# A hybrid decoder layer on one core: third buffers for a pair's operands, a later gate for the turned keys, and fewer small steps

## The chip, the cores and the metric

The kernel runs on one core of one Trainium2 chip. A core has TensorE (PE, with weight loads in a row of their own, PEld), VectorE (DVE), ScalarE (ACT), GpSimd (POOL) and SyncE (SP, which here issues nearly all DMAs). The metric is the device time of one execution in microseconds, the median of several runs; less is better. One further execution is profiled, and all rows come from it.

## The reference

One layer on 512 tokens of width 2048, all in f32. The input projection feeds three mixers side by side: differential attention (4 heads), sliding-window attention (8 query heads), and an RWKV-7 mixer (16 heads of 64). An output projection, a SwiGLU network of hidden width 5632 and a last norm follow. What the change touches is the RWKV recurrence:

```python
def step(S, inp):
    r_t, w_t, k_t, v_t, a_t, b_t = inp
    sa = jnp.einsum('bhvk,bhk->bhv', S, a_t)
    S = S * w_t[:, :, None, :] + sa[..., None] * b_t[:, :, None, :] + v_t[..., None] * k_t[:, :, None, :]
    return S, jnp.einsum('bhvk,bhk->bhv', S, r_t)
...
h = rms_norm(x, attn_norm_g[l]); proj = h @ w_in[l]
x = x + jnp.concatenate([ya, yb, yc], axis=-1) @ w_out[l]
gate, up = _split(rms_norm(x, ffn_norm_g[l]) @ w_gate_up[l], [FFN_HIDDEN, FFN_HIDDEN])
x = x + (jax.nn.silu(gate) * up) @ w_down[l]
```

## The kernel before

**Dense work.** Features lie on the partitions, the 512 tokens along the free dimension. A dense item is one output tile of 128 features: 16 k-tiles, each as three matmuls of 128x128 by 128x512 (high and low parts of both operands, type fp32r), 48 in all (`dense`, `dense_k`, L215 to L223). `sequence` (L348) runs the items in a fixed order and requests the weights of the next item before it runs one: two loads of 512 KB on SP, a split into high and low on ACT (L208) and DVE (L209). The order is r-, k- and v-tiles of eight head pairs (k first), the attention tiles, the output projection, the FFN.

**Small work.** The recurrence is done in chunks of 64 tokens, for a pair of heads (128 features) at a time. For pair `hp` these generators do it:

- `rates` (L457): decay and learning-rate tiles, from two small loads (`w2`, `a2`).
- `prep` (L494): norm of the keys (`kn`), the tile `bk` of scaled keys, the turned keys `bkn` (eight transposes, `bt`, L536 to L543), the tile `ar` with the scaled a and r operands (L547), the products `gr` (16 matmuls for each half of the chunks, L562), which DVE masks into `L`, `zl` and `gr` (L577); then four DMAs `li` (L588), the turned values `vt` (L598) and a bonus term `bon` (L609).
- `inverse` (L616): reads 32x32 triangular blocks back from DRAM and inverts them in 31 steps of two DVE operations, then writes them out (`xi`).
- `join` (L647): after a pause reads the inverted blocks into `L` (L653), after a second pause joins them by 32x32 matmuls (`px`, `pt`, `po`).
- `chain` (L688): eight chunks one after the other, each with small matmuls `z`, `u`, `S` (state) and `y`, and copies on ACT and DVE between them.
- `post` (L739): group norm (`var`), gate (`g`) and the store of the pair's output.

**The order.** All is planned when the program is written. Each generator stands in one of eight lanes, and `pump` (L163) is called after every dense matmul: it advances the first generator of each lane whose due time has come. `yield 7` means 7 planned microseconds; a bare `yield` means until the outputs of the step should be done, plus 0.3. `self.now` counts planned PE time. A wait for another generator is a loop that polls with bare yields. PE keeps exactly the order in which its instructions were written (`keep_in_program_order`); the other engines' instructions are ordered by a scheduler that keeps the dependencies. `need` (L181) pumps without dense work until a named generator is done.

**Buffers.** PSUM pool `pm` has two buffers (`kn`, `bt`, `gr`, `vt`, `bon`, scores), `pc` three, `py` one. In SBUF `ar`, `zl`, `gr`, `bkn`, `uv` and the inverse tiles `linv` exist twice. So `prep` of pair `hp` waits at L534 until the chain of pair `hp-2` has ended, before it turns the keys and goes on to `ar` and `gr`:

```python
while hp >= 2 and f"loop{hp - 2}" not in self.done:
    yield
bkn = rp.tile([P, NCH, P], F32, tag="bkn", name=f"bkn{hp}", bufs=2)
```

## Time and profile before

| | |
|---|---|
| runs, us | 2465.7, 2465.69, 2463.95 (median 2465.69) |
| profiled execution, us | 2460.77 |
| its span, us | 2459.0 |
| mean granted PE clock | 0.994 |
| mixers, to the first output projection | 0 to 805 us |
| output projection | 805 to 1000 us |
| FFN and last norm | 1000 to 2459 us |

The profile gives for each engine its busy time, and for each instruction its start, its length and what it waited for. "Waits" lists who waited for whom, with total, number and longest. "Windows" gives the busy time of the engines (and the number of their instructions) in stretches of time, with the granted clock of PE (1.00 is full), the DMA engines' share and GB/s. "Timeline" gives instructions in order of time: start, length, engine, line, operation, tiles, shapes, number; a bracket gives the idle time before and what ended it. In groups of instructions the columns are the number, the busy time, the mean in ns, and the idle time before. Matmuls are pipelined: their lengths overlap, and the distance of two starts is what one costs.

### The profile page before, as it was taken

What the parts mean: (1) busy time and instruction counts of PE and PEld (TensorE: products, weight loads), DVE (VectorE), ACT (ScalarE), POOL (GpSimd) and SP (SyncE); (2) the same over time, 40 slices, a digit from 0 to 9 for tenths busy, and PEclk for the clock granted to TensorE, in tenths of its full rate; (3) what the DMA queues carried; (4) which work ended last, traced back from release to release, by engine and by line L of the source; (5) the groups of instructions that cost most, each with busy time, mean ns of one, the idle gap of its engine ahead of it and who ended that gap; (6) DMA issues with size and microseconds to landing.
All of it is one profiled execution on the core that took longest, in us unless ns stands there. A gap on an engine that the chain in (4) does not pass through costs nothing.

```text
span 2459.0 us, 30832 instructions
## 1 busy us (share of the span) xinstructions
PE 2415.4 (98%) x12328; PEld 1915.2 (78%) x12328; DVE 1181.9 (48%) x2121; ACT 813.8 (33%) x1391; POOL 99.4 (4%) x157
## 2 busy tenths in 40 slices
PE   8999999999999999999999999999999999999997
PEld 6766666676677778888888888888888888888887
DVE  7567776675544544434343434343434333343437
ACT  5445555444434423322222122222222222222224
POOL 3000000000000003100000000000000000000006
PEclk9999999999999999999999999999999999999999
DMA  5222222222223433222322322322232232232224
GB/s 176 91 77 75 84 75 83 66 82 85 90 86 100 146 124 103 95 95 97 101 95 95 101 96 94 99 98 95 96 101 94 95 101 96 94 100 98 94 96 136
DMA packets 103793, 240.04 MB, mean 98 GB/s; under 512 B 34906, under 2 KB 43746, under 8 KB 103650
## 3 DMA queue, kind: packets, MB, share of 16 engines
q1 hardware_dynamic: 98754, 231.39, 29.4%
q10 hardware_dynamic: 4896, 6.69, 0.8%
q8 instruction: 97, 1.59, 0.3%
q14 instruction: 46, 0.38, 0.0%
HBM read 227.55 MB, written 10.49 MB: 97 GB/s over the span
## 4 chain that ended last, share of the span: by engine, by line
PE 87%; DVE 2%; ACT 1%; DMA 1%; issue 1%; SPq 0%; POOL 0%; DVEq 0%; ACTq 0%; POOLq 0%
PE pg L131 19%; PE pu L131 19%; PE pd L131 19%; PE po L131 7%; PE pd_v L131 3%; PE pd_k L131 2%; PE pd_r L131 2%; PE pd_va L131 2%; PE pd_qa L131 2%; PE pd_qb L131 2%; PE pd_ka L131 1%; PE y L131 1%; PE z L131 1%; PE S L131 1%; PE pd_kb L131 1%
## 5 line engine op out<-in xcount | busy, mean ns | idle before, releaser
L131 PE MATMUL pd<-al,wh_wd 128*128 128x512 f32 (+1 forms) x768 | 285.3, 371 | 0.6 <-DVE al L1141 0.6
L131 PE MATMUL pd<-ah,wh_wd 128*128 128x512 f32 (+1 forms) x768 | 285.5, 372 | 0.4 <-DVE y L1160 0.4
L131 PE MATMUL pd<-ah,wl_wd 128*128 128x512 f32 (+1 forms) x768 | 285.2, 371 | 0.0
L131 PE MATMUL pu<-x1h,wh_wu 128*128 128x512 f32 x704 | 274.3, 390 | 0.0
L131 PE MATMUL pu<-x1l,wh_wu 128*128 128x512 f32 x704 | 273.9, 389 | 0.0
L131 PE MATMUL pu<-x1h,wl_wu 128*128 128x512 f32 x704 | 273.9, 389 | 0.0
L131 PE MATMUL pg<-x1h,wl_wg 128*128 128x512 f32 x704 | 273.9, 389 | 0.0
L131 PE MATMUL pg<-x1l,wh_wg 128*128 128x512 f32 x704 | 273.9, 389 | 0.0
L131 PE MATMUL pg<-x1h,wh_wg 128*128 128x512 f32 x704 | 273.9, 389 | 0.0
L1160 DVE TENSOR_TENSOR y<-y,pd 128x512 f32<-128x512 f32 (+1 forms) x192 | 122.5, 641 | 207.8 <-PE pd L131 207.6
L208 ACT CAST wh_wd<-raw_wd 128x1024 fp32r<-128x1024 f32 x96 | 101.0, 1052 | 356.9 <-PE pd L131 177.2
L208 ACT CAST wh_wu<-raw_wu 128x1024 fp32r<-128x1024 f32 x88 | 92.7, 1053 | 366.7 <-PE pu L131 144.8
L208 ACT CAST wh_wg<-raw_wg 128x1024 fp32r<-128x1024 f32 x88 | 92.7, 1054 | 362.8 <-PE pg L131 144.9
L209 DVE TENSOR_TENSOR wl_wg<-raw_wg,wh_wg 128x1024 fp32r<-128x1024 f32 x88 | 107.8, 1225 | 171.4 <-ACT wh_wg L208 171.4
L209 DVE TENSOR_TENSOR wl_wu<-raw_wu,wh_wu 128x1024 fp32r<-128x1024 f32 x88 | 107.8, 1225 | 133.5 <-ACT wh_wu L208 133.5
L131 PEld LDWEIGHTS pd<-al,wh_wd 128*128 128x128 f32 x768 | 144.7, 188 | 25.7 <-DVE al L1141 0.8
L131 PEld LDWEIGHTS pd<-ah,wh_wd 128*128 128x128 f32 x768 | 144.7, 188 | 25.6 <-issue 0.5
L131 PEld LDWEIGHTS pd<-ah,wl_wd 128*128 128x128 f32 x768 | 144.7, 188 | 24.9
L131 PEld LDWEIGHTS pu<-x1h,wh_wu 128*128 128x128 f32 x704 | 132.1, 188 | 27.6 <-issue 0.2
L131 PEld LDWEIGHTS pu<-x1l,wh_wu 128*128 128x128 f32 x704 | 132.1, 188 | 27.6 <-issue 0.2
L131 PEld LDWEIGHTS pu<-x1h,wl_wu 128*128 128x128 f32 x704 | 132.1, 188 | 27.5
L131 PEld LDWEIGHTS pg<-x1h,wl_wg 128*128 128x128 f32 x704 | 132.1, 188 | 27.4
(357 smaller groups left out, 4100.4 us busy)
## 6 DMA issues: line engine op xcount, KB each, us to landing
raw_wd<-in_w_down SPq DMA_DIRECT2D x96, 512.0 KB, 3.2
raw_wg<-in_w_gate SPq DMA_DIRECT2D x88, 512.0 KB, 3.7
raw_wu<-in_w_up SPq DMA_DIRECT2D x88, 512.0 KB
raw_wo<-in_w_out SPq DMA_DIRECT2D x32, 512.0 KB, 3.5
raw_k<-in_w_in SPq DMA_DIRECT2D x16, 512.0 KB, 3.8
raw_r<-in_w_in SPq DMA_DIRECT2D x16, 512.0 KB, 4.3
raw_v<-in_w_in SPq DMA_DIRECT2D x16, 512.0 KB, 3.7
x<-in_xT SPq DMA_DIRECT2D x16, 256.0 KB, 4.9
```

The lines of the kernel that those rows point to most:

```text
L131: self.tc.keep_in_program_order(self.nc.tensor.matmul(out, lhsT, rhs, start=start, stop=stop))
L208: nc.scalar.copy(out=hi[:, :kn * m], in_=s)
L209: nc.vector.tensor_tensor(out=lo[:, :kn * m], in0=s, in1=hi[:, :kn * m].bitcast(F32), op=ALU.subtract)
L1160: nc.vector.tensor_tensor(out=o, in0=o, in1=ps, op=ALU.add)
```

## The change

- `ar` (a- and r-operands) and `zl` (the small chain's operand) become one tile `Z` with three planes, held three times; `gr` and `linv` are held three times too. The two ACT copies into `zl` go; DVE writes the a-operand in two halves.
- `prep` now forms `Z` and `gr` first. The keys are turned behind it, and wait only until the chain of `hp-2` has issued its last state matmul (`keys`, chunk 6); the values wait for that chain's end. With two keys blocks in one step, the gr half in one step without a pause in its middle, `bon` in the step of `vt`, and `g` in the step of `var`.
- `join` pauses 8 and 10 in place of 7 and 6.
- Waits are conditions that `pump` tests at its start, in place of polling. A chain starts only when its pair's `prep` has ended.
- Buffers: `w2`/`a2`/`rkm` three in place of four, `g2` one in place of two; `pts` shares a buffer with `xnn`; `keep` has its own; the attention's score tiles, its turned weights and the reloaded mixer outputs lie in `i2`, in a `gr` buffer and in `linv`.

```diff
+        for lane in self.order:
+            if lane:
+                name = lane[0][0]
+                if name in self.until and self.until[name]():
+                    del self.until[name]
+                    self.due[name] = self.now
+                self.due.setdefault(name, self.now)
...
-        self.linv = [lp.tile([P, NCH, P], F32, name=f"linv{j}") for j in range(2)]
+        self.linv = [lp.tile([P, NCH, P], F32, name=f"linv{j}") for j in range(3)]
...
-        while hp >= 2 and f"loop{hp - 2}" not in self.done:
-            yield
-        bkn = rp.tile([P, NCH, P], F32, tag="bkn", name=f"bkn{hp}", bufs=2)
-        for u in range(2):
-            ps = self.pm.tile([P, 4, P], F32, tag="m", name=f"bt{hp}_{u}")
-            for n in range(4):
-                self.tr(ps[:, n, :], bk[:, u * 4 + n].rearrange("p a c -> p (a c)"))
-            nc.scalar.copy(out=bkn[:, u * 4:u * 4 + 4, :], in_=ps)
-            yield
...
+        Z = rp.tile([P, NCH, 3, C], F32, tag="Z", name=f"Z{hp}", bufs=3)
+        for h in range(2):
+            s = HALF[h]
+            nc.vector.scalar_tensor_tensor(out=Z[s, :, h, :], in0=c3(kk)[s], scalar=-1.0, in1=W[s, :, 0:64],
+                                           op0=ALU.mult, op1=ALU.mult)
+        nc.vector.tensor_tensor(out=Z[:, :, 2, :], in0=c3(r), in1=W[:, :, 1:65], op=ALU.mult)
...
-                    self.mm(ps[h][:, j, :], bk[HALF[h], n], ar[HALF[h], n], start=True, stop=True)
-                if j == 1:
-                    yield 0.4
+                    self.mm(ps[h][:, j, :], bk[HALF[h], n], Z[HALF[h], n, h::2 - h], start=True, stop=True)
...
         self.lanes[1].append((f"sub{hp}", self.inverse(q)))
-        while "v" not in q:
-            yield
+
+        if hp >= 2 and f"keys{hp - 2}" not in self.done:
+            yield lambda: f"keys{hp - 2}" in self.done
+        bkn = rp.tile([P, NCH, P], F32, tag="bkn", name=f"bkn{hp}", bufs=2)
+        for u in range(2):
+            ps = self.pm.tile([P, 4, P], F32, tag="m", name=f"bt{hp}_{u}")
+            for n in range(4):
+                self.tr(ps[:, n, :], bk[:, u * 4 + n].rearrange("p a c -> p (a c)"))
+            nc.scalar.copy(out=bkn[:, u * 4:u * 4 + 4, :], in_=ps)
+        yield
+        q["bkn"] = bkn
+        if hp >= 2 and f"loop{hp - 2}" not in self.done:
+            yield lambda: f"loop{hp - 2}" in self.done
+        if "v" not in q:
+            yield lambda: not ("v" not in q)
...
-        yield 7
+        yield 8.0
         for h, b, bl in blocks:
             nc.sync.dma_start(out=L[bl, :, bl], in_=d[h, b].rearrange("n i g t -> (i g) n t"))
-        yield 6
+        yield 10.0
...
+                if n == NCH - 2:
+                    self.done.add(f"keys{hp}")
...
         nc.scalar.activation(sq, sq, AF.Exp, scale=-0.5)
-        yield
+        ps = self.pc.tile([P, T], F32, tag="c", name=f"g{hp}")
+        for j in range(2):
+            self.mm(ps, q["g2"][:, j, :], self.gl[j], start=(j == 0), stop=(j == 1))
         nc.vector.tensor_tensor(out=sq, in0=py, in1=sq, op=ALU.mult)
         self.done.add(f"y{hp}")
```

## The prediction

> **What bounds the kernel now.** I read the head of the page first. Its columns are busy time, share of the span, number of instructions.

> ```profile
> span 2459.0 us, 30832 instructions
> PE 2415.4 (98%) x12328; PEld 1915.2 (78%) x12328; DVE 1181.9 (48%) x2121; ACT 813.8 (33%) x1391; POOL 99.4 (4%) x157
> ```

> PE is the bound. PE runs in the order in which the program wrote its instructions, and the change leaves the number and shapes of the matmuls as they are. So the time can change in three ways only: PE's idle time, the clock at which PE runs, and the cost of switching between the long projection and the small steps. The chain that ended last gives the pace of undisturbed dense work, and where the untouched part begins:

> ```profile
> 1000.14 10.89 PE pg L131 x48
> ```

> 48 matmuls in 10.89 us are 0.227 us each. From 1000 us on the program is the same before and after; everything below lies in the first 1000 us. PE's waits (total, times, longest) are the second view:

> ```profile
> PE px L131 <- DMA linv<-xi: 9.7, 7, 2.9
> PE pd_l L131 <- ACT hl L311: 7.9, 3, 5.5
> ...
> PE bt L135 <- DVE bk L531: 2.3, 1, 2.3
> PE pd_k L131 <- DVE wl_k L209: 2.2, 1, 2.2
> ```

> pd_l is the loading at the start, which stays. The largest wait that the change can reach is px: the join of a pair waits for the inverted blocks to come back through DRAM. The third view, 50-us windows, ends each row with PEclk, the DMA share and GB/s:

> ```profile
> 50.00:100.00 50.00, 47.71 (x209) 38.19 (x208) 30.27 (x41) 29.88 (x43) 4.46 (x21) 1.00 0.26 83
> 100.00:150.00 50.00, 47.79 (x233) 36.60 (x231) 37.16 (x98) 21.17 (x32) 0.41 (x4) 1.00 0.30 91
> 150.00:200.00 50.00, 46.31 (x356) 32.00 (x355) 31.08 (x84) 25.37 (x63) 1.05 (x8) 0.93 0.26 73
> ...
> 450.00:500.00 50.00, 46.68 (x335) 32.80 (x333) 27.86 (x78) 24.34 (x54) 0.83 (x6) 0.90 0.25 69
> ...
> 550.00:600.00 50.00, 47.52 (x370) 32.39 (x369) 27.72 (x94) 22.51 (x62) 0.00 (x0) 0.97 0.29 89
> ```

> The three windows with a clock below 1.00 are those of the three long px waits. Lost: 50 x (0.07 + 0.10 + 0.03) = 3.5 + 5.0 + 1.5 = 10.0 us. The single waits of 2.3 us (bt) and 2.2 us (pd_k) lie in the first two windows and left the clock at 1.00. So px costs 9.7 + 10.0 us, and an idle stretch a little above 2.3 us is enough to lower the clock.

> **The change, part by part.**

> *The join's pauses, 7 and 6 to 8 and 10.* They are planned microseconds. On the first pair SP and PE show what they must cover (the last row is pair 7's):

> ```profile
> 150.73 2.64 SPq L642 DMA_DIRECT2D xi<-xy  x4
> 154.83 1.82 SPq L653 DMA_DIRECT2D linv<-xi  x4
> ```

> ```profile
> 156.67 0.28 PE L131 MATMUL px<-cc,linv 32*32 32x32 f32 x2 [2.95 <-DMA linv<-xi]
> 157.52 1.06 PE L131 MATMUL px<-cc,linv 32*32 32x32 f32 x30 [0.57 <-DMA linv<-xi]
> ...
> 582.27 1.04 PE L131 MATMUL px<-cc,linv 32*32 32x32 f32 x32 [2.37 <-DMA linv<-xi]
> ```

> The wait is 3.5 us at its worst and the plan gets 5 us more. I take all of px out, -9.7, and its clock, -10.0. Bounds: nothing of it, if the inverse ends later against the plan than now, to all of it. The join's four DMAs and its small matmuls come 5 us later; nothing but the pair's own chain waits for them, which today sits idle between pairs.

> *Merged steps.* A step between dense matmuls has an entry and an exit:

> ```profile
> 215.33 0.39 PE L131 MATMUL pd_k<-xl,wh_k 128*128 128x512 f32 x1
> 215.65 0.71 PE L131 MATMUL gr<-ar,bk 64*128 64x128 f32 x8
> 216.30 0.50 PE L131 MATMUL pd_k<-xh,wl_k 128*128 128x512 f32 x1
> 216.63 0.40 PE L131 MATMUL pd_k<-xh,wh_k 128*128 128x512 f32 x1
> ```

> Entry 0.32 - 0.227 = 0.09, exit 0.33 - 0.227 = 0.10: 0.2 us a switch. The gr steps lose 16 of them (3.2 us); the two bt steps and vt with bon lose one each per pair, at about 0.1 (a step of 128 rows enters without a pause): 1.6 us. Together -4.8 (rows of such a step at 328.95 to 329.53 below). Joining g to var I cost at nothing: four 512-column matmuls hide their switch.

> *The gate.* Now prep turns the keys (bt) before it forms gr, and bt waits until the chain of two pairs before has ended:

> ```profile
> 260.38 0.40 PE L131 MATMUL pd_k<-xh,wh_k 128*128 128x512 f32 x1
> ...
> 299.67 0.40 PE L131 MATMUL pd_r<-xh,wl_r 128*128 128x512 f32 x1
> ...
> 318.01 0.39 PE L131 MATMUL pd_k<-xh,wh_k 128*128 128x512 f32 x1
> ...
> 328.34 0.34 PE L131 MATMUL y<-gr,uv 128*64 128x64 f32 x4
> ...
> 328.95 0.39 PE L131 MATMUL pd_k<-xl,wh_k 128*128 128x512 f32 x1
> 329.18 0.60 PE L135 MATMUL bt<-cc,bk 128*128 128x128 f32 x4
> 329.53 0.48 PE L131 MATMUL pd_k<-xh,wl_k 128*128 128x512 f32 x1
> ...
> 406.72 0.69 PE L131 MATMUL px<-cc,linv 32*32 32x32 f32 x32
> ...
> 447.49 0.34 PE L131 MATMUL S<-uv,bkn 128*64 128x64 f32 x4
> ```

> These are pair 4 (k, its last r, its bt, its px, its seventh S), the next pair's k, and the last y of pair 2 that lets bt go. r was ready at 300, gr ended only at 346 (below). Behind the new gate gr would end some 12 us after r, near 312: some 30 us earlier, with four li DMAs on SP, the inverse and the chain behind it. That by itself buys nothing: PE has dense work meanwhile, and does the same work earlier.

> But it decides where bt stands. In the new order bt follows the last gr block, with a pause between only if the seventh S of the chain two pairs before isn't written yet. From gr's end to that S pass 447.49 - 346.14 = 101 us, with the join's pauses 106. Two pairs take 2 x (318.01 - 260.38) = 115 us. So the S is 9 us ahead, no pause is made, and bt stands on PE directly behind gr. Both use the two buffers of the PSUM pool pm. What bt then waits for:

> ```profile
> 345.49 0.72 PE L131 MATMUL gr<-ar,bk 64*128 64x128 f32 x8
> 346.14 0.50 PE L131 MATMUL pd_r<-xh,wl_r 128*128 128x512 f32 x1
> ```

> ```profile
> 346.24 0.42 DVE L577 TENSOR_TENSOR linv<-gr,cc 64x256 f32<-64x256 f32 x1 [0.49 <-PE gr L131]
> ...
> 347.13 0.42 DVE L577 TENSOR_TENSOR gr<-gr,cc 128x256 f32<-128x256 f32 x1
> ...
> 348.38 0.41 DVE L577 TENSOR_TENSOR gr<-gr,cc 128x256 f32<-128x256 f32 x1
> ```

> gr leaves PE free at 346.14. The first buffer is free after DVE's third operation, 347.55; four transposes take 0.35 (329.18 to 329.53); the second buffer is free at 348.79. So bt ends at 349.2, where it would have ended at 346.85 without the wait: **2.35 us** a pair, as two gaps of 1.4 and 0.9 us. Behind bt on PE is the dense stream. Pairs 0 and 1 have no gate and pay for sure; pairs 3 to 7 by the 9 us. Pair 2 I take to have its pause: chain 0 starts behind its px, at 157 now, and from px to the seventh S pass 41 us (406.72 to 447.49), while pair 2's gr no longer waits for that chain. 7 x 2.35 = +16.5. Bounds: two pairs, +4.7, up to seven with one weight split (1.22 us, next fence) ahead of them on DVE, +25.

> *The clock behind it.* The two gaps hold 2.3 us idle within 2.7, just where single waits of 2.2 and 2.3 us did nothing and 2.4 (the px of 582 us, whose clock fell least) did. I take a fall in four pairs at the smallest of the three, 1.5: +6.0. Bounds 0 and 7 x 5.0. [...]

> *vt waits for v.* vt now comes as soon as v's last operation is written down, by the plan some 0.45 us later (a pause of 0.3 and the next dense step), and that operation takes 0.75:

> ```profile
> L209 DVE TENSOR_TENSOR wl_r<-raw_r,wh_r 128x1024 fp32r<-128x1024 f32 x16 | 19.5, 1222 | 6.0 <-ACT wh_r L208 6.0
> ...
> L365 DVE SCALAR_TENSOR_TENSOR v<-h_v,cols,v 128x512 f32<-128x512 f32 x8 | 6.0, 746 | 0.0
> ```

> 0.3 x 6 pairs = +1.8; bounds 0 and 6 x 0.75 = 4.5.

> *At nothing:* the zl copies leave ACT, and one DVE operation of half height comes per pair; the page has both engines under half busy. Waits by condition in place of polling shift steps by at most 0.3 us. One g2 buffer makes its load wait for the g matmuls of the pair before, and the weight loads behind it on SP with it: they are issued a whole item of 10.9 us ahead, else each would cost PE that delay. The li DMAs, now earlier, meet other loads on SP; behind them only the inverse waits. The third buffers take away waits that planned pauses already cover, and the other renamed tiles change neighbours that are long done.

> **Sum:** -9.7 - 10.0 - 4.8 + 16.5 + 6.0 + 1.8 = **-0.2 us**. The profiled execution took 2460.8 us (2459.0 its span), 4.9 below the median of the runs, 2465.7; the difference is carried to the median: **2465.5 us**.

> **The rivals.**
> 1. *The clock falls behind every merged stall, at the mean of the three falls now* (3.3 us): 7 x 3.3 = 23.3 in place of 6.0. **Slower**, 2482.8 us. For it: little dense work stands around the gaps (gr, half the rows, before; transposes between). Against: two waits of 2.2 and 2.3 us left the clock alone. It decides from about 11 us of falls in all.
> 2. *The gate holds bt back*: chains run later than the 9 us allow, as DVE and SP serve them late; then pairs 2 to 7 have their pause, two pairs pay 4.7, one fall 1.5: -24.5 + 4.7 + 1.5 + 1.8 = -16.5, **2449.2 us**. For it: the margin is small against 106. Against: DVE is lighter when gr and inverse no longer crowd one another.
> 3. *px still waits*, because the inverse falls further behind the plan: 19.7 stay, **2485 us**. Against: 1.5 us of reserve even on the worst pair.
> 4. *Short gaps leave the clock alone*: the 6.0 go, **2459.5 us**. For it: the waits of 2.2 and 2.3 us. Against: the three falls. [...]
> 5. *The gate brings no earlier start* because r is late as well: then only px and merges count, the place of bt is that of rival 2, and so is the time.

> **Chances.** Forecast 0.40 (own range 2459 to 2472), rival 1 0.16, rivals 2 and 5 0.25, rival 3 0.07, rival 4 0.12. A measurement of this kernel can tell about 0.2%, 4.9 us, from no change. Faster: a quarter of the forecast's 0.40, nearly all of rivals 2 and 5, two thirds of rival 4: 0.10 + 0.24 + 0.08 = 0.42. Slower: 0.10 + 0.15 + 0.07 = 0.32. The rest, 0.26, is the same. The range goes from a little below rival 2 to rival 1: 2446 to 2483; rival 3 and the outer parts of 1 and 2 are left out, under 0.2.

> **What would show it.** px gone from PE's waits, or under 2 us; a new wait of bt on DVE's gr, some 14 to 17 us over seven pairs; PEclk of 1.00 at the joins and short dips behind gr; gr some 12 us behind r from pair 2 on; chain 7 ending before 600 us. If bt shows no such wait, or vt and gr show more than 5 us, the sum is wrong.

## The result and the profile after

| | before | after |
|---|---|---|
| median of the runs, us | 2465.69 (2463.95 to 2466.34) | 2451.97 (2451.28 to 2453.27) |
| profiled execution, us | 2460.77 | 2452.63 |
| its span, us | 2459.0 | 2450.8 |
| mean granted PE clock | 0.994 | 0.996 |

The changed kernel takes 0.9946 of the time before, 95% interval 0.9929 to 0.9963: 13.7 us less between the medians, 8.1 us between the two profiled executions. The forecast was 2465.5.

In the chain of the changed kernel that ended last (start, length, engine, tile) the FFN begins 8.3 us earlier:

```profile
991.84 10.89 PE pg L132 x48
```

From there to the end it is 2450.8 - 991.8 = 1459.0 us against 2459.0 - 1000.1 = 1458.9 before. So everything lies in the first part, as expected. PE's waits of the changed kernel (total, times, longest):

```profile
PE pd_l L132 <- ACT hl L321: 7.2, 2, 5.6
PE bt L136 <- DVE gr L574: 4.8, 3, 1.8
PE wt L136 <- DVE pa L891: 4.1, 5, 1.3
PE pa L132 <- ACT sg L385: 2.7, 4, 0.7
PE z L132 <- ACT uv L612: 2.1, 3, 1.1
PE bt L136 <- ACT bkn L596: 2.0, 3, 0.7
PE gr L132 <- DVE xt L645: 1.5, 2, 0.8
```

px is gone from the list. In its place stands bt behind DVE's gr, but three times and not seven. Below it are waits that weren't foreseen: z and pa of `rates`, which share the two buffers of `pm` with vt and bon (z waits until ACT has copied vt into uv, pa until ACT has read z's tile for sg), and the attention's turned weights wt behind DVE's pa (2.8 before). The windows, in the columns explained above:

```profile
100.00:150.00 50.00, 45.98 (x225) 35.84 (x224) 37.58 (x100) 19.09 (x30) 0.41 (x4) 0.97 0.26 79
150.00:200.00 50.00, 45.92 (x320) 33.98 (x317) 37.10 (x104) 23.50 (x47) 1.05 (x8) 0.93 0.30 85
...
450.00:500.00 50.00, 49.20 (x369) 33.97 (x367) 39.36 (x108) 29.36 (x65) 0.85 (x6) 1.00 0.23 70
...
550.00:600.00 50.00, 50.00 (x407) 34.63 (x407) 18.51 (x48) 24.98 (x73) 0.00 (x0) 1.00 0.24 75
```

The low clock at 450 to 500 and 550 to 600 us is gone with px. The first row is new: it holds pair 0's bt. PE's timeline there:

```profile
100.22 1.16 PE L132 MATMUL gr<-Z,bk 64*128 64x128 f32 x16
102.87 0.63 PE L136 MATMUL bt<-cc,bk 128*128 128x128 f32 x4 [1.49 <-DVE gr L574]
104.17 1.04 PE L136 MATMUL bt<-cc,bk 128*128 128x128 f32 x4 [0.68 <-ACT bkn L596]
104.86 0.78 PE L132 MATMUL pd_k<-xh,wl_k 128*128 128x512 f32 x1
```

bt stands directly behind gr and waits in two gaps, 1.49 + 0.68 = 2.17 us. The second is put down to ACT's copy of the first block, not to DVE. From 104.3 us on PE runs at half clock, as narrower windows show:

```profile
100.90:104.30 3.40, 1.24 (x15) 0.83 (x12) 2.87 (x7) 0.59 (x1) 0.00 (x0) 1.00 0.51 153
104.31:107.72 3.41, 3.41 (x11) 2.83 (x11) 0.00 (x0) 0.59 (x1) 0.00 (x0) 0.50 0.50 99
107.73:111.00 3.27, 3.27 (x18) 2.71 (x17) 0.16 (x1) 0.39 (x1) 0.00 (x0) 1.00 0.35 100
```

The fall lasts 3.41 us; in it the dense matmuls start 0.43 us apart, behind it 0.23, so about half of it is lost. Behind pair 1's bt it lasts twice as long, 6.83 us (152.09 to 158.91); behind pair 4's there is none (1.00 from 300 to 350 us).

**Where the time went.** I summed PE's gaps of over 0.06 us up to the FFN (those of pd_l at the start apart), half of the time at half clock, and took the remainder as work with its switches. Before: gaps 21.2, clock 10.2, work 960.3 us; after: 22.9, 5.1, 956.3. So gaps +1.7, clock -5.1, work -4.0, and 0.7 less of pd_l's gaps at the start: -8.1. PE hardly waits less than before; it waits in other places, in shorter gaps.

### The profile page after: what moved, and what is told of

It reads as the page before. It is cut to its first block, busy times and chain, and to the rows that moved or that the text cites. A ratio compares the mean times of both kernels' runs of the same rounds, so it can differ in the third digit from the quotient of the medians.

```text
span 2450.8 us, 30872 instructions
## 1 busy us (share of the span) xinstructions
PE 2406.4 (98%) x12328; PEld 1914.4 (78%) x12328; DVE 1184.6 (48%) x2129; ACT 808.1 (33%) x1375; POOL 100.0 (4%) x158
## 4 chain that ended last, share of the span: by engine, by line
PE 79%; DVE 2%; ACT 1%; issue 1%; POOL 0%; DMA 0%; DVEq 0%; ACTq 0%
PE pg L132 20%; PE pu L132 20%; PE pd L132 19%; PE po L132 7%; PE pd_ka L132 2%; PE pd_qa L132 2%; PE pd_va L132 2%; PE pd_qb L132 2%; PE pd_v L132 1%; PE pd_k L132 1%; PE pd_r L132 0%; PE y L132 0%; PE z L132 0%; PE pd_vb L132 0%; PE sb L132 0%
## 5 line engine op out<-in xcount | busy, mean ns | idle before, releaser
L132 PEld LDWEIGHTS pg<-x1h,wh_wg 128*128 128x128 f32 x704 | 132.1, 188 | 27.5
```

The source lines that it names most:

```text
L132: self.tc.keep_in_program_order(self.nc.tensor.matmul(out, lhsT, rhs, start=start, stop=stop))
```

## The experiments

The kernel before, on the same chips, had medians of 2467.0 us (first four runs below), 2467.2 (next four) and 2467.1 (last two). The ratios are to these. The changed kernel wasn't run again beside them; with it, the kernel before had 2465.7, so a difference to the changed kernel is good to some 1.5 us.

**1. The pauses alone.** The kernel before with the new pauses:

```diff
-        yield 7
+        yield 8.0
...
-        yield 6
+        yield 10.0
```

> The kernel before with one edit, the join's pauses 8 and 10. Theory A (the pauses hide the way through DRAM): PE's px waits fall from 9.7 us to under 1 and the clock stays at 1.00 at the joins, 10 to 20 us faster than before (2446 to 2456). Theory B (what ended the px waits in the changed kernel is the new order, which spreads the planned inverse): px still waits 4 us or more here, under 8 us faster.

2465.92 us, ratio 0.9990 (0.9979 to 1.0001): no change. A wait of its profile:

```profile
PE px L131 <- DMA linv<-xi: 6.6, 4, 3.9
```

Fewer px waits than the 9.7 us before, not none, and the granted clock was still 0.70 from 500 to 550 us and 0.98 from 550 to 600. So 5 us more of pause didn't cure px in the old order.

**2. The new order with the old pauses.** The changed kernel with 7 and 6:

```diff
-        yield 8.0
+        yield 7.0
...
-        yield 10.0
+        yield 6.0
```

> The changed kernel with the join's pauses back at 7 and 6. Theory A: px waits 5 us or more again and the clock falls at a join, 2457 us or more. Theory B: no px wait above 0.5 us, since in the changed kernel px stands 13 us or more behind the inverse's last operation and needs 7; the time stays at 2452, plus or minus 3.

2442.26 us, ratio 0.9903 (0.9887 to 0.9918): 9.7 us faster than the changed kernel. px isn't among its waits; bt is, less often:

```profile
PE pa L132 <- ACT sg L385: 3.4, 5, 0.7
PE bt L136 <- DVE gr L574: 3.3, 2, 1.8
...
PE bt L136 <- ACT bkn L596: 1.4, 2, 0.7
```

px is cured here without the pauses: the new order does it (which part of it, the third buffers or the later gate, no run separates). In the changed kernel px comes 13 to 38 us behind the inverse's last DVE operation, here 14 to 45, before 6 to 12; where it waited before, the way through DRAM took 6 to 8. The time was missed, because I expected the pauses to be neutral. They move every later step of a pair against the others: with the old ones pair 4's bt is held back and stalls no more. In the profiles PE's gaps are 6.6 us less, of which bt is 2.2 and wt behind pa 3.4, and the work 2.4.

**3. A pause ahead of bt.**

```diff
         self.lanes[1].append((f"sub{hp}", self.inverse(q)))
 
+        yield
         if hp >= 2 and f"keys{hp - 2}" not in self.done:
```

> The changed kernel with one bare pause between the last gr block and bt. Theory: bt waits on DVE and ACT (4.8 and 2.0 us in the changed kernel) go and with them the two clock dips behind gr of pairs 0 and 1 (3.4 and 6.8 us at half speed, 5.1 us lost), 8 to 12 us faster: 2440 to 2444. Rival (the dips would come with any gap in this stretch, and the waits move to vt or z): under 5 us faster.

2435.70 us (2435.37 to 2435.81), ratio 0.9874 (0.9857 to 0.9891): 16.3 us faster than the changed kernel, for one line. PE's timeline of pair 0 has no bracket any more, and the windows have full clock:

```profile
100.66 1.16 PE L132 MATMUL gr<-Z,bk 64*128 64x128 f32 x16
...
105.30 1.03 PE L136 MATMUL bt<-cc,bk 128*128 128x128 f32 x8
```

```profile
100.00:150.00 50.00, 48.47 (x243) 37.70 (x242) 40.14 (x108) 20.08 (x31) 0.41 (x4) 1.00 0.29 90
150.00:200.00 50.00, 49.49 (x386) 35.50 (x384) 39.67 (x111) 27.40 (x63) 1.16 (x9) 1.00 0.28 76
```

Gaps 10.6 in place of 22.9 us, clock 0 in place of 5.1. That is more than bt's own 6.8 + 5.1: some waits of z, pa and wt went too, as the steps behind moved.

**4. The steps unmerged.** The changed kernel with the pause back in the middle of a gr half, between the two keys blocks, and around bon:

```diff
                     self.mm(ps[h][:, j, :], bk[HALF[h], n], Z[HALF[h], n, h::2 - h], start=True, stop=True)
+                if j == 1:
+                    yield 0.4
...
             nc.scalar.copy(out=bkn[:, u * 4:u * 4 + 4, :], in_=ps)
-        yield
+            yield
```

> The changed kernel with the pauses inside gr, between the two bt blocks and around bon put back (g stays beside var). Theory (0.2 us a switch): 32 more switches, 4 to 5 us of PE time more; the bt waits lose their second part, 2 us. Together 1 to 5 us slower if the clock dips stay, so 2453 to 2457. Rival (switches cost nothing, PE's time is the sum of its matmuls): the same or 2 us faster.

2460.6 us, ratio 0.9970 (0.9960 to 0.9981): 8.6 slower than the changed kernel, more than expected. Not much of that is switches: in the profiles 27 more stretches of small steps between dense matmuls go with 1.3 us more work. px waits again, with the long pauses in place, and bt still stalls, in four pairs, though without the second gap:

```profile
PE bt L136 <- DVE gr L576: 6.7, 4, 2.2
PE px L132 <- DMA linv<-xi: 5.2, 2, 4.5
```

So this run doesn't price the merges alone. It shows again that px follows from where the plan puts the steps.

**5. bt behind gr in all pairs.** The wait for the keys of two pairs before now stands at the head of the step that forms `Z` and gr, so no pause can fall between gr and bt:

```diff
+        if hp >= 2 and f"keys{hp - 2}" not in self.done:
+            yield lambda: f"keys{hp - 2}" in self.done
...
         self.lanes[1].append((f"sub{hp}", self.inverse(q)))
 
-        if hp >= 2 and f"keys{hp - 2}" not in self.done:
-            yield lambda: f"keys{hp - 2}" in self.done
```

> The changed kernel with the wait for the chain of two pairs before moved ahead of Z and gr: no pause can fall between gr and bt any more, so bt stands directly behind gr in all eight pairs, as the prediction had it in seven. Theory A (the price in the prediction was right and only the number of pairs wrong): bt waits for gr and bkn about 2.17 us a pair, 8 x 2.17 = 17 us in all against 6.5 in the changed kernel, and the clock falls behind most of them, 1.5 to 3.4 us each, 10 to 20 us in all against 5: about 2452 + 10.5 + 10 = 2472 us, at least 2463. Theory B (the stall is smaller where DVE is free, or the clock seldom falls): under 10 us of bt waits, 2452 to 2458 us.

2493.82 us, ratio 1.0115 (1.0098 to 1.0132), the slowest of all. Its waits, and windows on the half-clock stretches behind the first four stalls:

```profile
PE bt L136 <- DVE gr L576: 17.7, 8, 3.0
...
PE bt L136 <- ACT bkn L596: 5.4, 8, 0.7
```

```profile
105.10:108.50 3.40, 3.40 (x11) 2.64 (x10) 0.00 (x0) 0.59 (x1) 0.00 (x0) 0.50 0.44 111
152.90:159.70 6.80, 6.12 (x19) 4.66 (x18) 0.74 (x2) 1.41 (x3) 0.73 (x5) 0.50 0.65 151
231.40:234.80 3.40, 3.20 (x11) 2.82 (x12) 0.00 (x0) 1.15 (x4) 0.00 (x0) 0.50 0.47 106
286.00:289.40 3.40, 3.40 (x10) 2.62 (x9) 2.19 (x12) 0.50 (x1) 0.00 (x0) 0.50 0.12 17
```

23.1 us of stall, 2.9 a pair, and a fall of the clock behind each of the eight, 41 us in all at half clock: 20.5 us lost, 2.6 a pair. The longest stall, 3.03 + 0.68, has a weight split of 1.22 us ahead of the masks on DVE, the upper bound of the prediction. Theory A holds, and 2472 was too low, for a reason that run 6 shows.

**6. The same gate, with the pause ahead of bt.** Run 5 with a bare `yield` where the wait stood.

> As e5_gate_ahead, with a pause of one planned step between gr and bt. Against e3_pause_before_bt (2435.7 us) it differs only in that gr, inverse and li loads of pairs 2 to 7 start when the chain of two pairs before has issued its seventh S, not before. If the early start of gr is worth nothing by itself (prediction: it buys nothing, PE has dense work meanwhile): 2434 to 2438 us, with no bt wait. If the early start is what keeps px and the chain from waiting: px waits come back, 5 to 20 us more, 2441 us or above.

2458.92 us, ratio 0.9968 (0.9959 to 0.9978). bt's waits fall to 2.9 us, and still it is 23.2 us slower than run 3, from which it differs only in the later start of gr, more than the 5 to 20 expected. On PE's timeline: one px wait, the last and the next dense matmul around a long stretch of small steps, and the end of the last chain; run 3's last y in the second fence:

```profile
207.52 1.32 PE L132 MATMUL px<-cc,linv 32*32 32x32 f32 x32 [4.77 <-DMA linv<-xi]
...
467.97 0.50 PE L132 MATMUL pd_v<-xh,wl_v 128*128 128x512 f32 x1
...
490.68 1.12 PE L132 MATMUL pd_qa<-xh,wh_qa 128*128 128x512 f32 x1
...
633.31 0.65 PE L132 MATMUL z<-uv,Z 128*64 128x64 f32 x4 [0.25 <-DVE uv L741]
...
638.23 0.70 PE L132 MATMUL y<-gr,uv 128*64 128x64 f32 x4 [0.29 <-ACT uv L730]
...
639.62 1.22 PE L132 MATMUL var<-ysq,cc 128*128 128x512 f32 x1 [0.69 <-ACT ysq L756]
```

```profile
588.26 0.34 PE L132 MATMUL y<-gr,uv 128*64 128x64 f32 x4
```

Against run 3 gaps are +11.0 and clock +17.1, and most of that stands in three places that run 3 doesn't have:

- The px wait costs some 11 us, 6.8 of them clock. It is pair 1's, whose own gr ends at 146.4 us in both runs: here too the plan has moved a join, and PE comes to it 4 us earlier.
- From 468 to 491 us PE has no dense matmul, and some 7 us go, 5.1 of them clock. As the program is written, nothing dense follows pair 7's v-tile until pair 6's values have been used (`need`).
- Chain 7 ends 50 us later, and its last chunks run with no dense matmul between them: each small wait on ACT or DVE is bare, and the clock falls there (10.2 us at half from 634.7 us on). Some 8 us go.

The early start of gr is worth those 23 us in this order of steps. In run 5 the dense matmuls stop in the same two places, from 489 to 517 and from 661 to 678 us. Run 5 is 34.9 us slower than this run; put down to its eight stalls alone, that is 4.4 us each.

**7. A pause in `rates`.** Run 3 with this:

```diff
-        if not hp:
-            yield 15.0
+        yield 2.5 if hp else 15.0
```

> e3_pause_before_bt with a planned pause of 2.5 us at the start of rates of pairs 1 to 7, where the matmuls z and pa found both buffers of pm still held by vt and bon (2.1 us behind ACT's uv and 2.7 us behind ACT's sg in the changed kernel). If these waits are of the same kind as the bt stall (PE reaches a step whose buffers are not read out yet): both go, 2 to 5 us less than e3, 2431 to 2434 us. If another wait takes their place: 2435 to 2437 us.

2434.86 us (2434.43 to 2436.15). z and pa wait no more, and a pd_k of 1.9 us behind a weight split has come in: no gain that the runs can tell.

**8. The attention's steps later as well.** Run 7 with `due.append(self.last + self.slack + 1.2)` in `diff_head`, and `yield 1.0` there ahead of the scores and of the turned values.

> e6_pause_in_rates with the attention's steps planned later as well: 1.2 us on the due times of its steps and 1 us ahead of the scores and of the turned values, where PE waited for DVE's pa, st and ACT in gaps of 0.5 to 1.3 us, some 8 us in all in the changed kernel. If PE's remaining gaps are worth what they show: 4 to 8 us less than e6, about 2427 us. If the later steps only push the output projection's inputs back: no gain, or a wait of po or the first output tile.

**2427.81 us** (2427.32 to 2429.28), ratio 0.9850 (0.9836 to 0.9864): 7.0 below run 7 on the same chip, and better than both kernels. PE's largest waits:

```profile
PE pd_l L132 <- ACT hl L321: 7.8, 3, 5.5
PE pd_k L132 <- DVE wl_k L219: 1.9, 1, 1.9
PE px L132 <- DMA linv<-xi: 0.9, 2, 0.5
```

wt, sa and p_van are gone. After the loading at the start the gaps up to the FFN are 4.2 us.

**9 and 10. Runs 3 and 8 with the old pauses**, 7 and 6, to see whether run 2's gain adds.

> e3_pause_before_bt (2435.7 us) with the join's pauses put back to 7 and 6. If the early gr is what keeps px from waiting and the longer pauses add nothing: no px wait over 0.5 us, 2434 to 2437 us. If e2_old_pauses was 10 us faster than the changed kernel because shorter pauses are better by themselves: 2425 to 2430 us. If the pauses cover what the early gr leaves open: px waits and clock falls, 2440 us or above.

> e7_best (2427.8 us) with the join's pauses put back to 7 and 6. Pauses without effect: 2426 to 2429 us; shorter pauses better by themselves: 2418 to 2424 us; px waiting: 2432 us or above.

2449.41 us, ratio 0.9930 (0.9916 to 0.9943), and 2449.80, ratio 0.9930 (0.9916 to 0.9944). They are 13.7 us slower than run 3 and 22.0 slower than run 8. Of PE's waits, first run 9, then run 10:

```profile
PE px L132 <- DMA linv<-xi: 6.7, 4, 4.3
```

```profile
PE px L132 <- DMA linv<-xi: 15.9, 5, 5.6
```

The pauses that added nothing in runs 1 and 2 are needed once bt has its own pause: in run 9 px comes 6 to 26 us behind the inverse's end, in run 2 14 to 45. Run 2's gain was not that shorter pauses are better.

## Why the prediction missed the gain

Its range held the time, its forecast was 13.5 us too high, and several terms were right for a different reason than given.

| term | forecast, us | in the profiled pair, us |
|---|---|---|
| px waits | -9.7 | -9.7 |
| clock behind px | -10.0 | -10.2 |
| merged steps (work) | -4.8 | -4.0 |
| bt behind gr | +16.5 | +6.8 |
| clock behind bt | +6.0 | +5.1 |
| vt waits for v | +1.8 | 0 |
| other waits, PE's start | 0 | +4.6, -0.7 |
| sum | -0.2 | -8.1 |

**The step that failed** is the one that set the number of stalls: from gr's end to the seventh S 101 us, with the pauses 106, against 115 for two pairs, "so the S is 9 us ahead, no pause is made". In the changed kernel that stretch takes 118 to 132 us in pairs 0 to 6 (97 in pair 7). The seventh S of two pairs before comes 20, 10, 6, 17 and 10 us after gr's end in pairs 2, 3, 5, 6 and 7; only in pair 4 it is ahead, by 6. For pair 4 SP and PE show why; gr ended at 329.90 - 1.49 = 328.4:

```profile
384.63 2.53 SPq L650 DMA_DIRECT2D xi<-xy  x4
...
389.35 1.79 SPq L661 DMA_DIRECT2D linv<-xi  x4
```

```profile
412.00 0.69 PE L132 MATMUL px<-cc,linv 32*32 32x32 f32 x32
...
454.13 0.34 PE L132 MATMUL S<-uv,bkn 128*64 128x64 f32 x4
```

From gr to px it is 83.6 us, where I had 60.6 + 5; from px to S 42.1, nearly as before (40.8). Of the 18 us more, 8 lie before the inverse's last operation and 10 behind it. px came 20.9 us after the last of these loads had been issued, and waited for nothing: the plan had put it there. I took the planned length of the inverse as fixed. But it is planned by how free the plan thinks DVE is, and in the new order the rest of prep's DVE work falls into it; that this is how it comes about is read from the program, not tried. The same shift gives px its reserve. So the two largest terms hang on one quantity: a late join cures px and holds bt back. I had credited the pauses with the first, which runs 1 and 2 refute for this kernel, and overlooked the second. In pairs 2, 3, 5, 6 and 7 bt has its pause. This is rival 2 with one pair more. That its 2449.2 is nearest to the time is in part luck: against the profiled -8.1 its -16.5 is as far off as the forecast's -0.2, and the median fell by more than the profiled pair for another reason (below). Of the signs that the prediction named, two more failed: gr ended 19 to 31 us behind r, not 12, and chain 7's last y stands at 604 us, not before 600.

**The price of a stall** was right: 2.17 us recorded in pairs 0 and 4 (2.5 in pair 1) against 2.35, in run 5 2.9 on average. Its second gap waits for ACT's copy, not DVE; the size is much the same.

**The clock behind it** fell in two of three stalls, by 1.7 and 3.4 us, where I had 1.5 in four of seven; that the sums, 5.1 and 6.0, are close is luck. Run 5, with a fall behind all eight at 2.6, sides with rival 1's mechanism: by its figures seven stalls would have cost 7 x (2.9 + 2.6) = 38 us, an estimate, more than the 24.5 us that the forecast took out, and the kernel would have been slower. I had read from single waits that a little over 2.3 us of idle lowers the clock; in the changed kernel the same two gaps, 1.49 and 0.68 us, were followed by a fall in pair 0 and by none in pair 4 (last section). Rival 4, by which short gaps leave the clock alone, doesn't hold: pair 0's fall to 0.50 follows just these.

**The median** moved by more than the profiled pair. The profiled execution before was a mild one, 4.9 us under its median, and I carried that difference over as fixed. It isn't: beside runs 1 to 4 the kernel before ran from 2460.3 us at a mean clock of 0.993 to 2472.6 at 0.988, while the changed kernel had 0.996 or 0.997 in all its runs. In the profiled pair 3.0 of the 8.1 us aren't clock; if that holds for the medians, some 10 of the 13.7 are (at 2466 us, 0.001 of clock is 2.5 us). Here waits that lower the clock now and then were dearer than one profile showed.

**"That by itself buys nothing"** was wrong of the early gr: run 6 against run 3 puts it at 23.2 us in this order of steps. I had reckoned that PE has dense work meanwhile. In run 6 it hasn't in two places, behind the last v-tile and at the end of the last chain, and a join that the plan has moved waits as well.

**Merges:** 33 stretches of small steps fewer (32 were reckoned) went with 4.0 us less work, 0.12 us each for entry and exit together; run 6 against the kernel before has 52 fewer and 7.8 us less, 0.15. In run 4 it was 0.05. The forecast's -4.8, 0.15 each on average, was close; its 0.2 for a gr step and 0.1 for the others weren't measured apart. **vt** never waits for v.

## What to carry to other kernels

Where the order of work is planned ahead, look at what a changed step does to the planned place of everything behind it before pricing the step itself: in the changed kernel one planned delay decided both whether px waits and how often bt stalls. A step that reads the buffers of the step before wants dense work between them (3.5 us of it in pair 0 of run 3, where no stall of bt is left). A later start on a path that looks idle can cost where the dense work runs out: in the middle, if the program holds the next tile back for it, and at the end of the stage, where nothing is left to hide its last link.

## What the runs showed of the hardware

The same gaps were followed by a fall in one pair and not in another. Those of bt, 1.49 and 0.68 us, lie in one stretch in pair 0 (above, 100.90 to 104.30 us, PE busy for 1.24 of 3.40). In pair 4 they are split between two, and the clock stays at 1.00:

```profile
329.90 0.63 PE L136 MATMUL bt<-cc,bk 128*128 128x128 f32 x4 [1.49 <-DVE gr L574]
331.20 0.65 PE L136 MATMUL bt<-cc,bk 128*128 128x128 f32 x4 [0.68 <-ACT bkn L596]
```

```profile
326.16:329.58 3.42, 2.25 (x24) 1.54 (x22) 1.10 (x3) 0.75 (x2) 0.22 (x3) 1.00 0.27 48
329.58:332.99 3.41, 2.42 (x14) 2.00 (x15) 1.34 (x4) 1.68 (x3) 0.00 (x0) 1.00 0.24 39
```

The single wait of 2.3 us of pair 0's bt in the kernel before shows the same. In the profile before it is split between two stretches, and the clock stays at 1.00; in run 1 the same wait lies in one, and the next 3.41 us are at 0.50. First the profile before, then run 1:

```profile
88.33:91.74 3.41, 2.15 (x10) 1.46 (x8) 3.37 (x5) 2.16 (x4) 0.11 (x1) 1.00 0.00 0
91.74:95.15 3.41, 2.38 (x15) 2.06 (x16) 1.66 (x3) 0.59 (x1) 0.00 (x0) 1.00 0.48 159
```

```profile
89.99:93.40 3.41, 1.17 (x7) 1.06 (x8) 2.87 (x4) 0.48 (x1) 0.00 (x0) 1.00 0.38 114
93.40:96.81 3.41, 3.41 (x11) 2.75 (x10) 0.00 (x0) 0.70 (x2) 0.00 (x0) 0.50 0.12 44
```

Against the program the borders stand at another place in run 1 than in the profile before (89.99 and 88.33 us above). The kernel before spread over 12.3 us in 23 runs, run 1 over 8.6 in 12. Run 3, at a mean clock of 0.998 in all its runs, repeats within 0.44 us in five; runs 7 and 8, at 0.998 in their profiles too, within 1.7 and 2.0 in four each. That the place of the borders is the cause of the spread is my estimate from these figures; no run tried it.
